# Layer 0 of a two-layer encoder trunk: the second half's squares, the logits' transposes and the first weight load are moved

## The chip, the cores and the metric

The kernel runs on one core of one Trainium2 chip. A core has five engines with a queue of instructions each: TensorE (PE in the profile; its weight loads are shown as PEld), VectorE (DVE), ScalarE (ACT), GpSimd (POOL) and SyncE (SP), which here issues the DMA loads. Each engine takes its queue strictly in order: an instruction that waits holds up all behind it. The metric is the device time of one execution in microseconds.

## The reference

The reference is a trunk of two layers over 1024 tokens of width 1024, all in float32. Layer 0 is the one that the change touches. Reduced to what matters here:

```
h     = rmsnorm(x, norm_mix_g[0])                 # needs the sum of squares of each token
proj  = h @ even_w_in                             # 28 blocks of 128 columns, and 8 logits per token
group A (RWKV-7): r, k, v, with token shift; decay, a and the gate g from low-rank products
                  g = sigmoid(xg @ g1) @ g2
group B (gated DeltaNet): q, k, v by a short convolution; gate
                  beta = sigmoid(logit 0..3);  g = -exp(a_log) * softplus(logit 4..7 + dt_bias)
mix   = concat(y_a, y_b) @ even_w_out
x     = x + mix; then a squared-ReLU MLP and a gated embedding
```

Layer 1 has windowed attention in place of the two groups. Nothing of what is computed changes.

## The kernel before

Activations lie transposed: 128 features on the partitions, tokens along the free axis. A product of full precision is made of three TensorE products of 128x128 by 128x512 each (high x high, high x low, low x high), so that a weight block of 128x1024 needs 8 x 3 = 24 matmuls for one half (HB = 512) of the tokens. `load_w` loads a weight (512 KB) into a buffer "wraw" (two of them), and `split_w` makes the two parts: a cast on ScalarE (L306) and a subtraction on VectorE (L307).

Layer 0 works in units. `layer0_in` lists 16 of them: for each half of the tokens, four pairs of an RWKV unit (two heads of group A) and a DeltaNet unit (one head of group B). Counted from 1, units 1, 3, 5, 7 of a half are RWKV and 2, 4, 6, 8 DeltaNet; the code counts u from 0. `l0_in` makes the input products of one unit after another. Its prologue, at u = 0 for the first half and u = 8 for the second, loads x, scales and splits it into `xg` (`split_scaled`, L355 and L356), sums its squares (`square`: ScalarE L666, and for all but the first tile an add on GpSimd L668), and then makes two low-rank products (`lora`) and the eight logits (`gdn_scalars`). In the first half the scaling by the token's norm is applied to the products when they are evacuated (`self.rs`), so that the first three products can begin before the norm is known; they lie in extra PSUM buffers until then.

`lora` mixes its weight on GpSimd twice (L700), splits both results, and makes two products. `gdn_scalars` loads the logits' weight, makes the product, evacuates it on VectorE (L717), transposes it on TensorE (L195) and computes beta and g with some two dozen small VectorE operations.

Behind the inputs, generators for `front`, `mid`, `back` and `post` of each unit (the lanes) are interleaved by `run`: it counts modelled time and asks next the lane that is due, with the estimates in `LAT`. `rwkv_front` and `gdn_front` make each unit's matrices; `inverse_start` sends the 16x16 diagonal blocks through memory to GpSimd, which inverts them in 28 small steps (L418, L420); `inverse_end` builds the full inverse on TensorE. A list scheduler then orders each engine's instructions: among those that its model holds ready it takes the one that stands first in the program, so that an instruction without early inputs can come much earlier in its queue than in the program.

The second half of x is needed twice: first for its sum of squares, in the program behind unit 7 (u == 6), then for the products of unit 9. The buffers for these loads, "ph" and "pl", hold two tiles each.

PSUM holds two buffers for these products (`bank`), taken in turn. The order in the program around the logits is: product of the logits, its transposes, first low-rank product of the gate (key "lg"), second.

## Time and profile before

| | us |
|---|---|
| median of 3 runs | 3081.69 |
| lowest and highest | 3079.91, 3084.43 |
| profiled execution | 3083.45 |
| its span on the core | 3081.7 |

| engine | busy us | share of the span |
|---|---|---|
| PE | 2969.4 | 96% |
| PEld | 2463.0 | 80% |
| DVE | 2233.0 | 72% |
| ACT | 1444.9 | 47% |
| POOL | 562.3 | 18% |

A row of a group or of the timeline names a line of the kernel, an engine and an operation, then the tile written and the tiles read (out<-in). In the timeline the first number is the start in us from the span's start, the second the duration, and the brackets at the end tell how long the engine had been idle and what ended that. In the view of waits each row gives who waited for whom, total us, how often, and the longest. A row of a line's own view gives shortest, median and longest duration in ns, and the first and last start. Layer 0's mixing takes about the first 900 us.

### The profile page before, as it was taken

To read this page: it belongs to the slowest core of one execution; us is meant where nothing else is said; L and a number is where in the kernel's file an instruction comes from. 1 tells how busy PE (TensorE), PEld (TensorE's weight loads), DVE (VectorE), ACT (ScalarE), POOL (GpSimd) and SP (SyncE) were. 2 spreads that over 40 slices of the span, in tenths; PEclk is the share of its full clock that TensorE was granted. 3 is DMA by queue.
4 is the path that set the end of the run, shared out by engine and by line. 5 is a ranking of instruction groups with operands and counts; after the bars stand their busy time and mean duration, and the time that the engine had idled before them with its cause. 6 is when DMAs were issued, how large, how long until landed. Compare 5 with 4: busy or idle time off the path is not lost.

```text
span 3081.7 us, 47201 instructions
## 1 busy us (share of the span) xinstructions
PE 2969.4 (96%) x17302; PEld 2463.0 (80%) x17302; DVE 2233.0 (72%) x4518; ACT 1444.9 (47%) x2824; POOL 562.3 (18%) x992
## 2 busy tenths in 40 slices
PE   7999999999999999999999989999999999999999
PEld 5777778777777888888888888989877888888887
DVE  6656766657848888878866677776868788878862
ACT  4333443334426544544433465666656544544431
POOL 6533542443500000000005111111200000000002
PEclk9999999999999999999999999999999999999999
DMA  4212112212346444754334111110256444754332
GB/s 139 71 54 62 55 55 74 62 53 64 120 158 215 160 154 149 252 174 149 126 101 131 55 44 41 49 55 27 78 190 227 144 154 150 258 168 152 124 109 99
DMA packets 190103, 362.18 MB, mean 118 GB/s; under 512 B 46272, under 2 KB 48560, under 8 KB 189872
## 3 DMA queue, kind: packets, MB, share of 16 engines
q1 hardware_dynamic: 161072, 306.73, 30.9%
q10 hardware_dynamic: 28800, 52.44, 4.4%
q8 instruction: 136, 2.23, 0.3%
q14 instruction: 95, 0.78, 0.1%
HBM read 265.71 MB, written 93.38 MB: 117 GB/s over the span
## 4 chain that ended last, share of the span: by engine, by line
PE 80%; DVE 9%; ACT 4%; DMA 3%; POOL 2%; issue 2%; SPq 0%; DVEq 0%; ACTq 0%; POOLq 0%
PE dps L180 66%; PE ch L180 2%; PE po L180 2%; PE pm L180 2%; PE pt L195 1%; PE iz L180 1%; PE sn L180 1%; PE tp L180 1%; DMA wraw<-in_w_qkv 1%; PE py L180 1%; POOL sub L420 1%; POOL subt L418 1%; PE pp L180 1%; DVE ptile L353 1%; DMA act<-in_w 1%
## 5 line engine op out<-in xcount | busy, mean ns | idle before, releaser
L180 PE MATMUL dps<-r,act 128*128 128x512 f32 x3528 | 829.1, 392 | 0.0
L180 PEld LDWEIGHTS dps<-r,act 128*128 128x128 f32 x3528 | 662.1, 188 | 145.7
L180 PE MATMUL dps<-xg,whi 128*128 128x512 f32 x1280 | 432.8, 418 | 14.2 <-ACT xg L355 7.3
L1617 POOL TENSOR_TENSOR pn<-pn,prs 128x512 f32<-128x512 f32 x32 | 46.9, 1468 | 1543.6 <-ACT prs L389 1449.0
L180 PE MATMUL dps<-wq,act 128*128 128x384 f32 x1536 | 305.4, 345 | 12.7 <-DVE vs L1879 7.1
L180 PEld LDWEIGHTS dps<-xg,whi 128*128 128x128 f32 x1280 | 233.5, 195 | 66.6 <-issue 8.0
L180 PEld LDWEIGHTS dps<-wq,act 128*128 128x128 f32 x1536 | 266.9, 191 | 16.0 <-DVE vs L1879 8.5
L180 PE MATMUL dps<-xg,wlo 128*128 128x512 f32 x640 | 258.0, 404 | 1.1 <-DVE wlo L307 1.1
L180 PE MATMUL dps<-late,act 128*128 128x512 f32 x960 | 229.2, 392 | 0.0
L180 PEld LDWEIGHTS dps<-late,act 128*128 128x128 f32 x960 | 180.3, 188 | 39.7
L1274 ACT CAST act<-act 128x512 fp32r<-128x512 f32 (+1 forms) x223 | 137.6, 648 | 130.9 <-PE dps L180 65.6
L1387 DVE TENSOR_TENSOR late<-late,dps 128x512 f32<-128x512 f32 x224 | 152.2, 684 | 56.1 <-PE dps L180 49.8
L1274 ACT CAST act<-late 128x512 fp32r<-128x512 f32 x210 | 124.3, 618 | 138.3 <-PE dps L180 94.7
L180 PE MATMUL dps<-act 128*128 128x512 f32 x672 | 165.0, 392 | 0.0
L1275 DVE TENSOR_TENSOR act<-act 128x512 fp32r<-128x512 f32 (+1 forms) x223 | 154.8, 722 | 5.2 <-ACT act L1274 5.1
L180 PEld LDWEIGHTS dps<-act 128*128 128x128 f32 x672 | 126.2, 188 | 28.6
L1275 DVE TENSOR_TENSOR act<-late,act 128x512 fp32r<-128x512 f32 x210 | 141.0, 688 | 8.9 <-ACT act L1274 7.0
L180 PEld LDWEIGHTS dps<-xg,wlo 128*128 128x128 f32 x640 | 124.1, 194 | 29.0 <-DVE wlo L307 1.6
L306 ACT CAST whi<-wraw 128x1024 fp32r<-128x1024 f32 x78 | 81.9, 1050 | 124.0 <-PE dps L180 79.8
L1525 DVE TENSOR_TENSOR xw<-xw,dps 128x512 f32<-128x512 f32 x174 | 118.0, 683 | 30.1 <-PE dps L180 27.8
L180 PE MATMUL dps<-xw,act 128*128 128x512 f32 x576 | 139.4, 392 | 0.0
L1392 ACT ACTIVATE late<-late 128x512 f32<-128x512 f32 x128 | 80.2, 629 | 112.5 <-DVE late L1387 107.7
(488 smaller groups left out, 5613.4 us busy)
## 6 DMA issues: line engine op xcount, KB each, us to landing
hb<-late ACTq DMA_DIRECT2D x168, 256.0 KB
act<-hb SPq DMA_DIRECT2D x138, 256.0 KB
late<-in_w SPq DMA_DIRECT2D x60, 512.0 KB
wraw<-in_w_in SPq DMA_DIRECT2D x56, 512.0 KB
act<-in_w SPq DMA_DIRECT2D x96, 256.0 KB
braw<-hb SPq DMA_DIRECT2D x72, 256.0 KB
wraw<-in_w_out SPq DMA_DIRECT2D x21, 512.0 KB
wraw<-in_w_qkv SPq DMA_DIRECT2D x21, 512.0 KB
```

The lines of the kernel that those rows point to most:

```text
L180: return self.begin(self.nc.tensor.matmul(out, lhsT, rhs, start=start, stop=stop, skip_group_check=again))
L195: return self.begin(self.nc.tensor.transpose(out, in_, ident))
L306: nc.scalar.copy(hi, raw)
L353: nc.vector.tensor_tensor(dst[:, 1, sl], src, dst[:, 0, sl].bitcast(F32), op=ALU.subtract)
L418: E.tensor_tensor(o, X[:, 0:i, i:i + 1].broadcast_to((NP, i, n)), Bq[:, i:i + 1, i + 1:16].broadcast_to((NP, i, n)), op=ALU.mult)
L420: E.tensor_tensor(X[:, 0:i, i + 1:16], X[:, 0:i, i + 1:16], o, op=ALU.add)
L1274: A.copy(hi, s)
L1275: V.tensor_tensor(lo, s, hi.bitcast(F32), op=ALU.subtract)
L1387: V.tensor_tensor(r, t, u, op=ALU.add)
L1392: A.activation(t, t, AF.Relu)
L1525: V.tensor_tensor(x[n][:, hs[hf]], x[n][:, hs[hf]], ps, op=ALU.add)
L1617: G.tensor_tensor(pn, pn, prs[:, sl], op=ALU.mult)
```

## The change

Four edits, all in the prologue of layer 0:

- The squares of the second half, which stood in the program behind unit 7, are spread: one load of two tiles and its two squares behind each of units 4 to 7 (u = 3 to 6). The load is pinned with `keep_in_program_order`, which draws an edge to the instruction traced last on its queue (SP), so that the scheduler can't issue it earlier. `load_x` gets an argument for that.
- `gdn_scalars` is cut in two. `gdn_logits` makes the product and its evacuation; the rest, from the transposes on, is called by `lora` between its first and its second product. The yield of "gdn_scalars0" goes.
- The first weight is loaded and split in two halves of its columns, 256 KB each: one before the first tile of x, one before the third.
- The loads of wa2, g2 and hv, and the exponential of a_log, come behind the three products of unit 1 in place of ahead of them.

```diff
                 if hf == 0:
                     acc = fr.tile([P, HB], F32, tag="rsbc", name="acc", bufs=2)
-                    self.w_first = self.load_w(a["w_in"][4])
+                    raw = self.wp.tile([P, 1024], F32, tag="wraw", name="wraw")
+                    self.w_first = [self.wp.tile([P, 1024], F32R, tag=f"w{q}", name=f"w{q}") for q in ("hi", "lo")]
+                    first = iter([slice(0, HB), slice(HB, T)])
...
                 for k in range(NK):
                     if hf == 0:
+                        if k % 2 == 0 and k < 4:
+                            c = next(first)
+                            nc.sync.dma_start(out=raw[:, c], in_=a["w_in"][4][:, c])
+                            self.split_w(raw[:, c], HB, [z[:, c] for z in self.w_first])
                         xr = self.t2()
                         nc.sync.dma_start(out=xr, in_=a["x"][k, :, 0:HB])
...
                 for f in squares:
                     f()
+                sc = {}
                 if hf == 0:
+                    rsc = self.sm.tile([P, 4], F32, tag="rsc", name="rsc")
+                    self.rs = fr.tile([P, HB], F32, tag="rsbc", name="rsbc", bufs=2)
+
+                    self.extra = [lambda t=t: self.psm.tile([P, HB], F32, tag=t, name="dps") for t in ("y", "ch", "pm")]
+                    self.late, self.plan = [], {2: lambda: self.row_stats([acc], rsc), 3: lambda: self.to_rows(rsc, self.rs)}
+                    raws = yield from getattr(self, nm + "_in")(p, hf, u)
                     self.wa2 = fr.tile([P, 512], F32, tag="wa2", name="wa2")
                     nc.sync.dma_start(out=self.wa2, in_=a["wa2"])
...
                     nc.scalar.activation(self.ea, self.hv[:, 0:1, :], AF.Exp)
-                sc = {}
-                if hf == 0:
-                    rsc = self.sm.tile([P, 4], F32, tag="rsc", name="rsc")
...
-                    raws = yield from getattr(self, nm + "_in")(p, hf, u)
...
             self.mark(("in", u), 1.0)
-            if u == 6:
-
-                acc = fr.tile([P, HB], F32, tag="rsbc", name="acc", bufs=2)
-                for q in range(4):
-                    x2 = self.load_x(q, self.pre, "pl" if q % 2 else "ph")
-                    for e in range(2):
-                        self.square(acc, x2[:, e], q + e == 0)
+            if 3 <= u < 7:
+
+                q = u - 3
+                if q == 0:
+                    acc = fr.tile([P, HB], F32, tag="rsbc", name="acc", bufs=2)
+                x2 = self.load_x(q, self.pre, "pl" if q % 2 else "ph", True)
+                for e in range(2):
+                    self.square(acc, x2[:, e], q + e == 0)
...
             if u % 8 == 0:
 
-                yield from self.gdn_scalars(hf, sc)
-                gg = yield from self.lora(1, [(0, 128, 2)], "lg")
+                ba = yield from self.gdn_logits()
+                gg = yield from self.lora(1, [(0, 128, 2)], "lg", lambda: self.gdn_scalars(hf, sc, ba))
...
-    def load_x(self, q, pool, tag):
+    def load_x(self, q, pool, tag, keep=False):
 
         x2 = pool.tile([P, 2, HB], F32, tag=tag, name="xr")
-        self.nc.sync.dma_start(out=x2, in_=self.a["x"][2 * q:2 * q + 2, :, HB:T].rearrange("k p t -> p k t"))
+        load = self.nc.sync.dma_start(out=x2, in_=self.a["x"][2 * q:2 * q + 2, :, HB:T].rearrange("k p t -> p k t"))
+        if keep:
+            self.tc.keep_in_program_order(load)
         return x2
...
-    def lora(self, i, mus, key):
+    def lora(self, i, mus, key, between=None):
...
         yield from self.dense_half(wa, lambda ps: nc.vector.tensor_tensor(out, ps, self.rs, op=ALU.mult))
+        if between is not None:
+            between()
         sb = yield from self.project(wb, key, 1)
...
-    def gdn_scalars(self, hf, sc):
-        nc, a, l0 = self.nc, self.a, self.l0
+    def gdn_logits(self):
+        nc, a = self.nc, self.a
...
         yield from self.dense_half(self.split_w(raw), lambda ps: nc.vector.tensor_tensor(ba[0:8, 0:HB], ps[0:8], self.rs[0:8],
                                                                                          op=ALU.mult))
-        yield "gdn_scalars0"
+        return ba
+
+    def gdn_scalars(self, hf, sc, ba):
+        nc = self.nc
         pt = self.bank()
```

4 lines of the change are left out of this document (removed).

## The prediction

> **What bounds the kernel now.** I read the page first, then a table of stretches around the one hole that the 40 slices show, then the waits of TensorE, then the rows around the hole.
>
> ```profile
> span 3081.7 us, 47201 instructions
> PE 2969.4 (96%) x17302; PEld 2463.0 (80%) x17302; DVE 2233.0 (72%) x4518; ACT 1444.9 (47%) x2824; POOL 562.3 (18%) x992
> ```
>
> TensorE works 96% of the span, so time is to be had only where it stands still or runs at half clock. The next table (columns: stretch, length, busy time of PE, PEld, DVE, ACT, POOL, granted clock, DMA share, GB/s) splits the 900 us of layer 0.
>
> ```profile
> 0.00:7.31 7.31, 0.00 (x0) 0.00 (x1) 1.24 (x4) 3.00 (x4) 6.33 (x58) 1.00 0.68 205
> 7.31:18.07 10.76, 9.33 (x27) 6.78 (x27) 8.87 (x11) 10.76 (x19) 10.14 (x23) 1.00 0.96 357
> 18.07:46.48 28.41, 28.41 (x130) 23.35 (x130) 15.10 (x22) 10.77 (x16) 22.09 (x20) 1.00 0.26 76
> 49.55:58.30 8.75, 0.00 (x2) 0.00 (x1) 7.50 (x19) 4.22 (x7) 5.38 (x5) 0.62 0.75 232
> 65.54:80.00 14.46, 13.03 (x68) 10.14 (x69) 7.25 (x29) 4.34 (x14) 0.50 (x1) 0.88 0.26 78
> 80.00:350.00 270.00, 261.39 (x2267) 200.92 (x2266) 171.27 (x377) 104.10 (x211) 121.66 (x270) 0.97 0.21 64
> 350.00:900.00 550.00, 526.14 (x4442) 407.47 (x4443) 365.00 (x831) 211.54 (x445) 217.14 (x471) 0.95 0.24 76
> ```
>
> Three idle places stand out: 7.31 us before the first matmul, 1.43 us inside the next 10.76, and 8.75 us in one piece from 49.55. The remaining 820 us of the layer hold 8.6 + 23.9 = 32.5 us, in crumbs. TensorE's waits of the first 90 us name what ended them:
>
> ```profile
> PE dps L195 <- DVE f L717: 8.7, 1, 8.7
> PE dps L180 <- ACT xg L355: 7.3, 1, 7.3
> PE dps L180 <- DVE wlo L307: 0.9, 1, 0.9
> ```
>
> The long wait is for the logits' evacuation (L717); the transposes of its result (L195) block TensorE's queue. The timeline around it, all engines mixed, shows why L717 is late:
>
> ```profile
> 39.10 1.83 POOL L668 TENSOR_TENSOR acc<-acc,xr 128x512 f32<-128x512 f32 x1
> 43.90 1.35 DVE L307 TENSOR_TENSOR wlo<-wraw,whi 128x1024 fp32r<-128x1024 f32 x1 [2.14 <-ACT whi L306]
> 46.51 1.26 POOL L668 TENSOR_TENSOR acc<-acc,xr 128x512 f32<-128x512 f32 x1
> 47.73 1.89 POOL L700 TENSOR_TENSOR wraw<-lraw,vecs 128x1024 f32<-128x1024 f32 x1
> 49.65 1.05 ACT L306 CAST whi<-wraw 128x1024 fp32r<-128x1024 f32 x1 [1.20 <-POOL wraw L700]
> 50.73 1.33 DVE L307 TENSOR_TENSOR wlo<-wraw,whi 128x1024 fp32r<-128x1024 f32 x1 [5.47 <-ACT whi L306]
> 57.57 0.67 DVE L717 TENSOR_TENSOR f<-dps,rsbc 8x512 f32<-8x512 f32 x1
> 58.30 0.59 PE L195 MATMUL dps<-ident,f 8*128 8x8 f32 x4 [8.75 <-DVE f L717]
> ```
>
> The logits' product was over by 46.48. VectorE stood idle for 5.47 us, not on L717 but on the weight split queued ahead of it (L307), which waits for ScalarE's cast, which waits for GpSimd's mixing of the second low-rank weight (L700), which stood behind a square sum of the second half (L668, acc<-acc,xr). After L307 VectorE works through unit 1's front until 57.57.
>
> **The change part by part.** Sums go against the profiled execution, 3083.45 us (its span 3081.7); the median of the three runs, 3081.69, is 1.76 lower.
>
> *First weight in halves.*
>
> ```profile
> 1.25 0.42 SPq L300 DMA_DIRECT2D wraw<-in_w_in  x1
> 3.58 0.20 POOL L241 TENSOR_SCALAR d_omu<-vecs 128x12 f32<-128x12 f32 x1
> 5.59 1.04 ACT L306 CAST whi<-wraw 128x1024 fp32r<-128x1024 f32 x1 [3.50 <-DMA wraw<-in_w_in]
> 6.54 0.72 ACT L355 ACTIVATE xg<-f,vecs 128x512 fp32r<-128x512 f32 x1
> 18.07 0.50 PE L180 MATMUL dps<-xg,wlo 128*128 128x512 f32 x1 [0.89 <-DVE wlo L307]
> 27.24 1.23 DVE L307 TENSOR_TENSOR wlo<-wraw,whi 128x1024 fp32r<-128x1024 f32 x1 [6.99 <-ACT whi L306]
> L666 ACT ACTIVATE xr<-xr x7: 613/617/633, 17.7 to 45.1; 128x512 f32<-128x512 f32 x7
> ```
>
> 512 KB took 4.3 us from issue (1.25) to cast (5.59). The 81.5 KB of the vectors, issued at 0.80, were used by 3.58, so 2.8 us. Between the two, 256 KB take about 3.4: the half lands near 4.7, 0.9 early. Its cast, half as wide, is near 0.62 (the row of ScalarE's 128x512 squares) for 1.04: 0.4 early. So the first matmul moves from 7.31 to about 6.0. Against it: two casts of 0.62 take 0.2 more of ScalarE, which has no idle time from 7.31 to 18.07 (10.76 busy of 10.76), and one more issue of 0.42 stands before the later x tiles. Bounds: a loss of 0.6, a gain of 2.5 (more than half of the 4.3 cannot go). The lead meets the fourth product's weight, whose split ends at 28.47; TensorE comes to it near 29.5 (24 matmuls a product at 0.227 us from 18.07, and 1 us of statistics), so about 1 us passes. I take **-1.0**.
>
> *wa2, g2, hv and the exponential behind unit 1's three products.* Three issues of 0.33 us on SP's queue leave the place ahead of the second weight and go ahead of the first low-rank load, which is in any case held to 18.04 by a buffer. The first reader of wa2 is at 46.60:
>
> ```profile
> 18.04 0.34 SPq L692 DMA_DIRECT2D lraw<-in_lora  x1
> 46.60 1.78 PE L180 MATMUL tp<-lao,wa 64*128 64x512 f32 x4
> ```
>
> Some 30 us cover a transfer; without that cover it would cost about its 3.4 us. Sum: **0**; the second weight comes some 2 us earlier, but its cast stands behind ScalarE's full queue.
>
> *Squares away from the start.* The eight squares of the second half leave ScalarE (8 x 0.62) and GpSimd (seven adds), and their loads SP's queue, where unit 2's weights stood behind them.
>
> ```profile
> L668 POOL TENSOR_TENSOR acc<-acc,xr x7: 1257/1305/2126, 35.2 to 51.0; 128x512 f32<-128x512 f32 x7
> L831 DVE TENSOR_SCALAR f<-f x8: 426/460/1404, 52.1 to 744.8; 128x512 f32<-128x512 f32 x8
> ```
>
> L700's second part can start 1.2 us earlier (the add at 46.51), and up to 3 if the add at 39.10 (1.83) goes from ahead of L700's first half, at 40.88, too. L831, the step between tanh and scan, lost 0.94 (1.404 against a median of 0.460) under the adds at 49.71. All of that lies ahead of L717.
>
> *Transposes behind the gate's low-rank product.* TensorE meets the 24 matmuls of that product first. Their weight is split by 45.25 (43.90 + 1.35), so they fill 24 x 0.227 = 5.45 us of the hole. Also, the product no longer needs the logits' PSUM buffer, which L717 holds. Left of the hole: 8.75 - 5.45 - (1.2 to 3) = 2.1 to 0.3; I take 1.2, so **-7.55**. What is late next is still L717, then the second low-rank product behind the transposes. The half-clock stretch after the hole goes as well:
>
> ```profile
> 58.82 1.22 PE L180 MATMUL dps<-xg,whi 128*128 128x512 f32 x2
> 61.55 0.79 PE L180 MATMUL dps<-xg,whi 128*128 128x512 f32 x2
> 62.18 0.39 PE L180 MATMUL dps<-xg,wlo 128*128 128x512 f32 x1
> 62.41 0.62 PE L180 MATMUL dps<-xg,whi 128*128 128x512 f32 x2
> ```
>
> From 58.82 to 61.95 seven matmuls start 0.43 apart, then 0.227 apart: 3.13 - 7 x 0.227 = **-1.5**. Does a 1.2 us rest of the hole keep a slow stretch alive? After the 1.43 us wait at 69.03 the row of 65.54:80.00 shows a clock of 0.88, which is (1 - 0.88) x 14.46 / 0.5 = 3.5 us at half speed, so here a short wait among small products was enough; kept, such a stretch would cost 1.7, and the time would be 1.7 higher. The Trainium skill, "TensorE: Matmul & The Clock Gate", Part 1, says that the gate halves the clock only after an idle window of some 3.4 us; by that rule the whole 1.5 is gained. The page and the 0.88 row differ, and the first hole, with its 0.62, suits both. I take the 1.5, since the matmuls now ahead are dense ones.
>
> The price: the second low-rank product now takes the PSUM buffer that the first one's evacuation has just to free, with only the 0.59 us transposes between.
>
> ```profile
> L706 DVE TENSOR_TENSOR lgo<-dps,rsbc x1: 683/683/683, 69.2 to 69.2; 128x512 f32<-128x512 f32 x1
> ```
>
> 0.68 + queueing - 0.59: from 0.1 to about 1.2 when L724 and a few of the gate's small VectorE steps are ahead; **+0.5**. In the second half (L717 at 460.6) other lanes' matmuls fill it: 0. The gate's scalars come 5.45 us later there and here; their reader, unit 2's front, comes after four more products (22 us), so 0.
>
> *Squares in units 4 to 7.* Each unit gets one load on SP's queue, two ScalarE squares and two GpSimd adds, beside the 16x16 inverses that GpSimd does. How much room has the inverse?
>
> ```profile
> 106.13 0.40 ACT L445 ACTIVATE T<-Xp,half 128x128 f32<-128x128 f32 x1 [6.42 <-DMA Xp<-z]
> 126.79 0.24 PE L180 MATMUL iz<-T,N 32*32 32x16 f32 x6
> 345.25 0.35 ACT L445 ACTIVATE T<-Xp,half 128x64 f32<-128x64 f32 x1 [0.45 <-DMA Xp<-z]
> 345.66 0.44 PE L180 MATMUL iz<-T,Ng 32*32 32x16 f32 x32
> ```
>
> Unit 1's result waits 20 us for TensorE, unit 6's none. Bounds: nothing (GpSimd is busy 121.66 of 270), and 4 x 2 x 1.305 = 10.4 if every add delays an inverse that TensorE awaits. Nearest is the row of the 270 us with 8.6 us of PE idle in all: I take a tenth, **+1.0**.
>
> Sum: -1.0 - 7.55 - 1.5 + 0.5 + 1.0 = -8.55; 3083.45 - 8.55 = 3074.9; on the footing of the median, **3073.1**.
>
> **The rivals.**
> *The hole moves on.* The products run ahead but the recurrent lanes do not, and TensorE waits later, where unit 6 has no room. For it: the pair of rows at 345. Against it: 20 us of room at unit 1, and GpSimd's chain moving up too. What stays is what the lanes gain (1.2 to 3 from L700, 0.94 from L831, say 3), the start's 1.0, less 1.5: 3081.69 - 2.5 = 3079.2.
> *Slower: GpSimd's adds hold up the inverses.* At units 4 to 7 each pair of adds takes up to 2 x 2.13 = 4.26 us, in the middle of the chain of 28 small steps; four of them, all awaited, are 17.0. Less the 9.55 of the other terms: 3081.69 + 7.5 = 3089.2. It decides from 15.7 us of delay on (3.9 a unit). Against it: the median add is 1.305, and unit 1's inverse has 20 us of room.
> *The pin doesn't hold*, and the squares still come early: the product fills 5.45, 3.3 us are left: -1.0 - 5.45 - 1.5 + 0.5 = -7.45, so 3074.2, inside the forecast.
>
> **How the numbers follow.** Forecast (with the pin's rival) 0.65, hole moves on 0.20, slower 0.13, still faster by more than 17 us 0.02. A change of 0.2% (6.2 us: 3075.5 and 3087.9) is about what a measurement of this kernel can tell from none. The forecast's own range is 3067 to 3077: all of the 8.75, 1.5 and 2.5 gained, or the start at its loss and a slow stretch kept. A new order of layer 0 can move its 32.5 us of crumbs by a few us either way, so it opens to 3065, and to 3084 to hold the second case; above that lies most of the slower one. Faster 0.66, same 0.21 (a hundredth of the forecast falls short of 3075.5), slower 0.13.
>
> **What would show it.** Right: first matmul near 6.0; no wait of TensorE above 2.5 us between 45 and 60, the low-rank product ahead of the L195 transposes; acc<-acc,xr on GpSimd only from about 150 us on; PE idle from 80 to 900 us within 4 us of 32.5. Wrong: waits for iz or T growing between 180 and 450, inverses stretched by adds, ScalarE waiting for an x tile in units 4 to 7.

## The result, and the profile after

The changed kernel is slower. Its median is 3095.16 us (3086.16 to 3105.72, nine runs) beside 3081.09 us for the kernel before (3075.65 to 3085.21, nine runs); the ratio is 1.0047, with a 95% interval of 1.0032 to 1.0061. The forecast was 3073.1, with a range of 3065 to 3084. All medians here and below are of fast executions; a slow one, of the kernel called before_squares below (10343 us at a mean granted clock of 0.497), is left out, and as it was the traced one, no trace of that kernel is read.

The page of the changed kernel, its span and its row of engines:

```profile
span 3093.3 us, 47222 instructions
PE 2980.7 (96%) x17302; PEld 2465.8 (80%) x17302; DVE 2233.5 (72%) x4519; ACT 1442.9 (47%) x2825; POOL 552.7 (18%) x992
```

Set this beside the rows of before. TensorE executes the same 17302 matmuls, and its idle time is the same: 3081.7 - 2969.4 = 112.3 us before, 3093.3 - 2980.7 = 112.6 after. Of the 11.6 us between the spans 11.3 are *busy* time. The same matmuls took longer, which is the mark of a lower granted clock, not of a wait.

The early part did most of what was forecast. The waits of TensorE in the first 80 us of the changed kernel (who waited for whom, total us, times, longest):

```profile
PE dps L179 <- ACT xg L354: 6.9, 1, 6.9
PE dps L194 <- DVE f L726: 2.3, 1, 2.3
...
PE dps L179 <- DVE wlo L306: 1.0, 1, 1.0
```

The hole of 8.75 us is down to 2.3. The timeline shows the low-rank product ahead of it and what comes after it:

```profile
54.38 0.39 PE L179 MATMUL dps<-xg,wlo 128*128 128x512 f32 x1
54.61 0.95 PE L179 MATMUL tp<-hsel,f 128*128 128x2 f32 x8
57.81 0.41 PE L194 MATMUL dps<-ident,f 8*128 8x8 f32 x4 [2.26 <-DVE f L726]
58.15 0.73 PE L179 MATMUL dps<-xg,whi 128*128 128x512 f32 x2
```

Where the time went is read from a table by stretches (length; busy time of PE, PEld, DVE, ACT, POOL; granted clock; DMA share; GB/s): the start, the rest of the first half's early units, the rest of layer 0, and layer 1 with the end. Before:

```profile
0.00:80.00 80.00, 60.85 (x262) 47.51 (x263) 46.86 (x94) 35.46 (x63) 52.55 (x110) 0.91 0.42 134
80.00:330.00 250.00, 241.90 (x2101) 187.08 (x2101) 156.35 (x347) 95.52 (x194) 106.33 (x235) 0.97 0.21 63
330.00:920.00 590.00, 565.20 (x4709) 437.68 (x4708) 391.44 (x882) 228.03 (x474) 232.47 (x505) 0.95 0.25 80
920.00:3065.00 2145.00, 2090.80 (x10190) 1782.28 (x10189) 1634.18 (x3190) 1084.36 (x2092) 169.63 (x141) 0.99 0.40 134
```

After:

```profile
0.00:80.00 80.00, 66.22 (x299) 50.90 (x300) 50.03 (x98) 34.27 (x60) 43.43 (x109) 0.98 0.32 101
80.00:330.00 250.00, 237.82 (x2008) 183.02 (x2008) 152.74 (x325) 92.39 (x187) 104.68 (x232) 0.91 0.22 66
330.00:920.00 590.00, 563.30 (x4722) 434.61 (x4718) 385.30 (x887) 225.65 (x476) 236.54 (x510) 0.95 0.25 79
920.00:3065.00 2145.00, 2090.41 (x10185) 1778.75 (x10184) 1638.50 (x3201) 1087.62 (x2098) 162.97 (x139) 0.99 0.40 135
```

Idle time is length less PE's busy time; time at half clock is (1 - clock) x length / 0.5. A us at half clock loses some 0.43 us among small matmuls (an estimate from clock_micro below, where 25.8 us of work took 44.6 to 46.8). So:

| stretch | idle, after less before | half clock, after less before | worth, us |
|---|---|---|---|
| 0 to 80 | 13.8 - 19.2 = -5.4 | 3 - 14 = -11 | -5.4 - 4.8 = -10.2 |
| 80 to 330 | 12.2 - 8.1 = +4.1 | 45 - 15 = +30 | +4.1 + 12.9 = +17.0 |
| 330 to 920 | 26.7 - 24.8 = +1.9 | 59 - 59 = 0 | +1.9 |
| 920 to 3065 | 54.6 - 54.2 = +0.4 | 43 - 43 = 0 | +0.4 |

The sum is +9.1 for a measured +11.6; the rest lies within what the clock's two decimals can hide. By this estimate the start gained 10 us, about what the prediction had for it, and the stretch from 80 to 330 us, where units 2 to 6 are at work, gave back 17, three quarters of it as half clock. The question is what put them there.

### The profile page after: what moved, and what is told of

Same layout as the page of the kernel before. It is cut to its first block, busy times and chain, and to the rows that moved or that the text cites. A ratio compares the mean times of both kernels' runs of the same rounds, so it can differ in the third digit from the quotient of the medians.

```text
span 3093.3 us, 47222 instructions
## 1 busy us (share of the span) xinstructions
PE 2980.7 (96%) x17302; PEld 2465.8 (80%) x17302; DVE 2233.5 (72%) x4519; ACT 1442.9 (47%) x2825; POOL 552.7 (18%) x992
## 4 chain that ended last, share of the span: by engine, by line
PE 81%; DVE 10%; ACT 3%; DMA 2%; issue 2%; POOL 2%; SPq 0%; ACTq 0%; DVEq 0%; POOLq 0%
PE dps L179 68%; PE ch L179 2%; PE po L179 2%; PE iz L179 1%; PE pt L194 1%; PE pm L179 1%; PE sn L179 1%; PE tp L179 1%; DVE wlo L306 1%; DVE ptile L352 1%; PE py L179 1%; DMA wraw<-in_w_qkv 1%; DVE f L1072 1%; POOL subt L417 1%; POOL sub L419 0%
## 5 line engine op out<-in xcount | busy, mean ns | idle before, releaser
L179 PEld LDWEIGHTS dps<-wq,act 128*128 128x128 f32 x1536 | 264.8, 189 | 17.0 <-DVE vs L1891 10.2
L305 ACT CAST whi<-wraw 128x1024 fp32r<-128x1024 f32 (+1 forms) x79 | 81.7, 1034 | 115.8 <-PE dps L179 79.6
```

Source lines behind the costliest of these rows:

```text
L179: return self.begin(self.nc.tensor.matmul(out, lhsT, rhs, start=start, stop=stop, skip_group_check=again))
L305: nc.scalar.copy(hi, raw)
```

## The experiments

The theories were these. **A**: the work of the squares in units 4 to 7 costs the time itself, either the GpSimd adds between the steps of the inverses (A1) or the loads and ScalarE's squares (A2). **B**: the new order of layer 0's instructions costs it, whichever edit brings the order about. **C**, formed later, is how B could cost so much: a short wait ahead of a stretch of small matmuls leaves that whole stretch at half clock. In what follows W is the first weight in halves, M the moved loads of wa2, g2 and hv, L the logits' transposes behind the low-rank product, S the squares in units 4 to 7. Ratios are to the kernel before, with their 95% intervals.

| kernel | contains | median, us | ratio |
|---|---|---|---|
| after | W M L S | 3095.16 | 1.0047 [1.0032, 1.0061] |
| after_no_squares | W M L | 3072.87 | 0.9978 [0.9965, 0.9991] |
| after_no_logits | W M S | 3102.85 | 1.0077 [1.0060, 1.0094] |
| before_logits | L | 3071.83 | 0.9979 [0.9961, 0.9998] |
| before_squares | S | 3104.54 | 1.0081 [1.0061, 1.0101] |
| before_halves | W | 3095.96 | 1.0050 [1.0028, 1.0072] |
| before_moves | M | 3087.73 | 1.0027 [1.0016, 1.0039] |
| after_no_adds | W M L S less the adds | 3084.42 | 1.0011 [0.9994, 1.0028] |
| after_adds_on_vector | adds on VectorE | 3082.76 | 1.0005 [0.9991, 1.0018] |
| after_loads_only | the loads and one square | 3077.23 | 0.9992 [0.9977, 1.0006] |
| after_unpinned | S without the pin | 3072.60 | 0.9975 [0.9959, 0.9991] |
| unpinned_again | the same | 3074.75 | 0.9979 [0.9964, 0.9995] |
| early_squares | S right behind unit 1 | 3087.87 | 1.0021 [1.0007, 1.0036] |
| dummy_adds | unpinned, and nine adds | 3084.28 | 1.0018 [1.0002, 1.0034] |

The kernel before had medians of 3078.3 to 3081.1 beside them.

### One part away, one part alone

**after_no_squares** puts the squares back behind unit 7, without the pin:

```diff
-            if 3 <= u < 7:
-                q = u - 3
...
-                x2 = self.load_x(q, self.pre, "pl" if q % 2 else "ph", True)
...
+            if u == 6:
+                acc = fr.tile([P, HB], F32, tag="rsbc", name="acc", bufs=2)
+                for q in range(4):
+                    x2 = self.load_x(q, self.pre, "pl" if q % 2 else "ph")
...
```

> The changed kernel with its squares put back: one block in the program behind unit 7, loads not pinned; the other three edits stay. Theory A (the pinned squares hold up GpSimd's inverses of units 2, 4 and 6, which took 6.5 to 10 us longer in the changed kernel): the loss goes with them, and the time falls to the kernel before or below it, 3070 to 3083. Theory B (any new order of layer 0 interleaves unit 3's front with unit 2's inverse and leaves TensorE runs of small matmuls, at half clock for 109 us of layer 0 against 85; the squares aren't the cause): it stays slow, 3088 to 3100, with more than 100 us at half clock.

**after_no_logits** takes the logits' part back:

```diff
-                ba = yield from self.gdn_logits()
-                gg = yield from self.lora(1, [(0, 128, 2)], "lg", lambda: self.gdn_scalars(hf, sc, ba))
+                yield from self.gdn_scalars(hf, sc)
+                gg = yield from self.lora(1, [(0, 128, 2)], "lg")
```

> The changed kernel with the logits' transposes back ahead of the gate's low-rank product; the other three edits stay. Theory A: as slow as the changed kernel or slower, since the squares stay, 3090 to 3102, and TensorE's hole near 50 us, 2.3 us in the changed kernel, is back at about 5 us (8.75 less the 1.2 to 3 of the absent squares). Theory B: the order changes again, so anything from 3078 to 3100; if the dense products' run ahead at 60 to 120 us is what starves later stretches, then 3078 to 3086.

**before_squares** and **before_logits** make these two edits alone in the kernel before (the same lines, the other way round).

> The kernel before with the pinned squares alone. Theory A: slower by 8 us or more, 3089 to 3098, with the inverses of units 2, 4 and 6 stretched. Theory B: within 6 us of before unless its order happens to change, and 3 us faster where the hole near 50 us shrinks with GpSimd's earlier low-rank weight.

> The kernel before with the logits' transposes behind the gate's low-rank product alone. Theory A: faster, 3072 to 3078: the hole of 8.75 us shrinks to about 3.3 and no square touches an inverse. Theory B: the products run ahead as in the changed kernel, later stretches lack them, and the gain is lost again: 3080 to 3095 with more time at half clock than the 85 us of before.

The squares are the loser and the logits the winner. With W, M and L the kernel takes 3072.87, within 0.3 us of the forecast for the whole change; that is in part luck, since the terms of W and L were not met one by one (see "Why the prediction was wrong"). The squares add 22.3 us to that (3095.16 - 3072.87), and alone about 25 (0.81% of 3080; 19 to 31). The logits' part gains 7.8 us alone (3079.62, the kernel before beside it, less 3071.83; by the interval of its ratio 0.6 to 12) and 7.7 in the company of the others (3102.85 - 3095.16).

The page of after_no_squares:

```profile
span 3065.3 us, 47212 instructions
PE 2961.1 (97%) x17302; PEld 2451.1 (80%) x17302; DVE 2227.9 (73%) x4519; ACT 1444.3 (47%) x2825; POOL 557.6 (18%) x992
```

This execution is 6 us below its kernel's median, so the sizes are rough. Idle 104.2 against 112.6 with the squares, busy 2961.1 against 2980.7: of 28.0 us between the two spans 8.4 are waiting and 19.6 are clock.

### What of the squares costs it

**after_adds_on_vector** and **after_no_adds** give `square` an engine for its sum, VectorE (`nc.vector`, shown here) or none (`None` in its place), for the second half alone (without the adds the sum of the squares is missing from the second half's norms):

```diff
-                    self.square(acc, x2[:, e], q + e == 0)
+                    self.square(acc, x2[:, e], q + e == 0, nc.vector)
```

> The changed kernel with the seven adds of the pinned squares on VectorE in place of GpSimd (0.68 us each there, 1.27 on GpSimd). Theory A1 (GpSimd is the contended engine: seven adds of 1.27 between the steps of the inverses, and VectorE slowed beside them): most of the 22 us that the squares cost goes, 3073 to 3082. Theory A2 (the loads' place on SP's queue or ScalarE's squares do it): 3090 to 3100. Theory B (a new order by itself costs or wins some 10 us): anything from 3075 to 3100.

> The changed kernel with those seven adds left out altogether (the second half's sum of squares then holds one tile of eight); loads and ScalarE's squares stay. Theory A1: as without the squares, 3070 to 3080, and the inverses of units 2, 4 and 6 take 28, 23 and 20 us again. Theory A2: 3090 to 3100.

**after_loads_only** keeps the four pinned loads and the first square (the second half's norms then hold one tile of eight):

```diff
                 for e in range(2):
-                    self.square(acc, x2[:, e], q + e == 0)
+                    if q + e == 0:
+                        self.square(acc, x2[:, e], q + e == 0)
```

> The changed kernel with the four pinned loads and one square alone; the other seven squares and the adds are left out (the second half's sum of squares then holds one tile of eight). Theory A1: 3070 to 3080. Theory A2 by the loads (each waits on SP's queue and holds up weights or the inverses' transfers behind it): 3090 to 3100; by ScalarE's squares: 3070 to 3080 here and 3090 to 3100 without the adds. Theory B: anything from 3070 to 3095, and not in step with what is left out.

**after_unpinned** lets the scheduler put the loads where it likes:

```diff
-                x2 = self.load_x(q, self.pre, "pl" if q % 2 else "ph", True)
+                x2 = self.load_x(q, self.pre, "pl" if q % 2 else "ph")
```

> The changed kernel with the same loads and squares in the same places of the program, but not pinned. The scheduler can then issue the first two loads early again, as in the kernel before. If the place in the queues costs: 3070 to 3080, with the first squares on GpSimd before 60 us. If the place in the program alone reorders layer 0: 3085 to 3100.

Taking the adds off GpSimd takes 12.4 us off the 22, leaving them out 10.7, and leaving out the other seven squares too another 7.2. The pinned loads with one square are still 4.4 above after_no_squares. A1 accounts for half, then, by this reading. The inverses do get stretched: the 28 steps on GpSimd that begin at 128 us take 26.8 us, for 20.6 in the unpinned kernel (from 126 us on), and those that begin at 233 us take 23.6, for 19.9 (from 221 us on). GpSimd in the changed kernel, with the adds (L675) among the steps of unit 4's inverse (L417, L419):

```profile
249.39 0.57 POOL L417 TENSOR_TENSOR subt<-sub,subb 32x36 f32<-32x36 f32 x1
249.93 1.27 POOL L675 TENSOR_TENSOR acc<-acc,xr 128x512 f32<-128x512 f32 x1
251.17 0.70 POOL L419 TENSOR_TENSOR sub<-sub,subt 32x36 f32<-32x36 f32 x1
...
251.97 1.27 POOL L675 TENSOR_TENSOR acc<-acc,xr 128x512 f32<-128x512 f32 x1
```

TensorE a little later:

```profile
258.42 0.62 PE L194 MATMUL pp<-ident,fr 128*128 128x128 f32 x4 [2.02 <-DVE fr L1197]
...
262.25 0.63 PE L179 MATMUL iz<-T,Ng 32*32 32x16 f32 x32 [2.21 <-ACT T L444]
262.81 2.07 PE L179 MATMUL tp<-AR,b 64*128 64x128 f32 x14
```

The same operations in the unpinned kernel, where TensorE doesn't wait:

```profile
250.41 0.38 PE L179 MATMUL iz<-T,Ng 32*32 32x16 f32 x24
250.72 1.16 PE L179 MATMUL tp<-AR,b 64*128 64x128 f32 x14
```

The wait for that inverse is 2.21 us, and the 14 transposes behind it take 2.07 us in place of 1.16. Stretched inverses were one of the signs that the prediction had named as wrong. Their waits are small beside 22 us, though, and the second effect, the slow matmuls, is not in the prediction's price for it. Nor do the adds alone make this wait: in early_squares (below), without an add near, TensorE waits 1.33 us at the same place.

The unpinned kernel also shows the rival in which the pin doesn't hold. Its squares run at 37 to 53 us, as before; those of the changed kernel run at 132 to 350. First the unpinned kernel's line of the adds, then the changed one's:

```profile
L675 POOL TENSOR_TENSOR acc<-acc,xr x7: 1274/1289/2155, 37.0 to 52.9; 128x512 f32<-128x512 f32 x7
```

```profile
L675 POOL TENSOR_TENSOR acc<-acc,xr x7: 1254/1272/1289, 132.1 to 350.4; 128x512 f32<-128x512 f32 x7
```

With its 3072.6 the unpinned kernel beats both.

### The squares elsewhere, other work in their place, and the weight alone

**early_squares** keeps pin and squares, but puts all four loads behind unit 1's gate product:

```diff
                 self.mark(("lg", hf))
+                if hf == 0:
+                    acc = fr.tile([P, HB], F32, tag="rsbc", name="acc", bufs=2)
+                    for q in range(4):
+                        x2 = self.load_x(q, self.pre, "pl" if q % 2 else "ph", True)
+                        for e in range(2):
+                            self.square(acc, x2[:, e], q + e == 0)
```

> The changed kernel with all four pinned loads and their squares right behind the gate's second low-rank product of unit 1, not in units 4 to 7. GpSimd has 10 us of idle time there (69.8 to 78.4 us in the changed kernel, before the first inverse) and no inverse is under way. Theory A1 (the squares cost because of where they meet the inverses and unit 3's and later fronts; out of the way of the low-rank weight they shorten the hole of 5.6 us near 56 us to 2.3): 3066 to 3072, below every kernel so far. If the squares cost wherever they are pinned: 3078 to 3095.

**dummy_adds** takes the unpinned kernel and gives GpSimd nine adds that nothing needs, behind units 4 to 7:

```diff
+            if 3 <= u < 7:
+                if u == 3:
+                    dum = fr.tile([P, 384], F32, tag="dum", name="dum")
+                    nc.gpsimd.memset(dum, 0.0)
+                for j in range(3 if u == 6 else 2):
+                    nc.gpsimd.tensor_tensor(dum, dum, raws[j][:, 0:384], op=ALU.add)
```

> The changed kernel without the pins (3072.6, squares early), plus nine adds of 128x384 on GpSimd that nothing reads, two or three behind each of units 4 to 7, each waiting for that unit's own products: about 9 us of GpSimd work in the places of the pinned adds, with no load and no ScalarE square. Theory A1 (GpSimd's time among the inverses is the main price, some 11 of 22 us): 3080 to 3088. If the pinned adds cost only together with the loads and squares that they wait for: 3070 to 3076.

**before_halves** is the first weight in two halves, alone in the kernel before:

```diff
-                    self.w_first = self.load_w(a["w_in"][4])
+                    raw = self.wp.tile([P, 1024], F32, tag="wraw", name="wraw")
...
+                        if k % 2 == 0 and k < 4:
+                            c = next(first)
+                            nc.sync.dma_start(out=raw[:, c], in_=a["w_in"][4][:, c])
+                            self.split_w(raw[:, c], HB, [z[:, c] for z in self.w_first])
```

> The kernel before with the first weight loaded and split in two halves, alone. The prediction's term is 1.0 us gained. The traces of the changed kernels show the first matmul at 6.8 to 7.3 us for 7.31, but the second product's wait for its weight ending at 18.2 to 18.9 for 18.07, so the expectation now is no gain: within 4 us of before, 3077 to 3085.

The dummy adds cost 11.7 us (3084.28 - 3072.60), as A1 asks. The other two do not fit it. The early squares have their adds at 103 to 115 us, none in units 4 to 7, and are still 15 us above the unpinned kernel. And the halved weight, which puts nothing at all among the lanes, costs 15 us alone (0.50%; 0.28 to 0.72%). Its row of engines:

```profile
PE 2988.2 (96%) x17302; PEld 2472.4 (80%) x17302; DVE 2231.3 (72%) x4519; ACT 1445.0 (47%) x2825; POOL 555.1 (18%) x992
```

Its span is 3099.8, so it idles 111.6 us, 0.7 less than before, and is busy 18.8 longer. TensorE's instruction order differs from that of before from 25.5 us on, though only the first load was touched, since the list scheduler works out every queue anew. So there the order alone did it, by way of the clock.

Taken over ten of the profiles, busy time goes with the mean granted clock, for the same 17302 matmuls: 2961.1 at 0.982 (after_no_squares), 2965.5 at 0.980 (after_unpinned), 2969.4 at 0.978 (before), 2974.0 at 0.976 (after_adds_on_vector), 2978.4 at 0.975 (after_no_adds), 2980.7 at 0.974 (after), 2987.2 at 0.973 (after_no_logits), 2988.2 at 0.972 (before_halves). Two of the others stand off this line, 2968.0 (before_logits) and 2978.1 (early_squares), both at 0.977.

### Is it the clock, and what sets it?

One place gave the hint. The same run of 232 small and dense matmuls of the lanes took 18.2 us at full clock in the unpinned kernel (from 249.66 us on) and 31.3 us, nearly all of it at half clock, in early_squares (from 255.18 us on), where a 1.33 us wait stood shortly ahead of it. The next runs asked whether that is the cause, whether slow places belong to the order, and whether an edit without any work shifts the time.

**clock_micro** is a kernel of its own: dense matmuls, a wait for a chain of VectorE operations, then a stretch of small ones:

```diff
+        for turn in range(3):
+            for waits in (0, 1, 2, 4):
+                d = dense(60)
+                first = raw
+                if waits:
+                    first = sb.tile([P, HB], F32, tag="chain", name="chain", bufs=2)
+                    nc.vector.tensor_scalar(first, d, 0.5, None, op0=mybir.AluOpType.mult)
+                    for _ in range(waits - 1):
+                        nc.vector.tensor_scalar(first, first, 0.5, None, op0=mybir.AluOpType.mult)
+                lanes(8, first)
```

> This kernel computes nothing of the trunk; it only measures the clock. Twelve turns (0, 1, 2 and 4 chained 128x512 VectorE operations, three times over): 60 dense 128x512 matmuls, then TensorE waits for the chain, then some 216 small matmuls like those of the lanes, with no further wait. Theory C (a stretch of small matmuls keeps the clock that it enters with, and a wait of 1 to 3 us ahead of it is enough to enter slow): turns without a wait run their small matmuls at a clock of 1.0; turns with the longer waits run them at 0.5 for most or all of the stretch, so that the same stretch takes up to 1.7 times as long; dense matmuls bring the clock back. Rival D (the clock follows the kind of matmul, not the wait): all twelve stretches show the same clock. Rival E (only idle time above some 3 us counts): stretches behind waits of up to 2.6 us show 1.0, all of them.

Four of its waits in the timeline, of three sizes:

```profile
60.49 0.37 PE L17 MATMUL pm<-raw,chain 64*128 64x128 f32 x1 [0.78 <-DVE chain L61]
...
101.36 0.37 PE L17 MATMUL pm<-raw,chain 64*128 64x128 f32 x1 [1.25 <-DVE chain L63]
...
143.13 0.37 PE L17 MATMUL pm<-raw,chain 64*128 64x128 f32 x1 [2.17 <-DVE chain L63]
...
283.86 0.37 PE L17 MATMUL pm<-raw,chain 64*128 64x128 f32 x1 [1.24 <-DVE chain L63]
```

The stretches behind them, and the first one, without a wait:

```profile
20.15:45.86 25.71, 25.71 (x434) 23.55 (x433) 0.00 (x0) 0.00 (x0) 1.00 0.01 3
60.49:86.27 25.78, 25.78 (x433) 23.62 (x433) 0.00 (x0) 0.00 (x0) 1.00 0.01 2
101.36:127.13 25.77, 25.77 (x433) 23.62 (x433) 0.00 (x0) 0.00 (x0) 1.00 0.01 2
143.13:187.77 44.64, 44.64 (x433) 40.85 (x433) 0.00 (x0) 0.00 (x0) 0.53 0.01 1
...
283.86:329.23 45.37, 45.37 (x433) 41.58 (x433) 0.00 (x0) 0.00 (x0) 0.52 0.01 1
```

The same 432 small matmuls take 25.8 us or 45 us. There is nothing between: the clock is 1.00, or 0.50 to 0.53 for the stretch. Of three stretches each, none was slow behind no wait, none behind 0.78 us, one behind 1.24 us, and all three behind 2.17 us. Each slow stretch had TensorE busy for all of its 45 us, and the clock came back only 1.3 to 4.2 us into the dense matmuls that followed. So rivals D (the kind of matmul alone) and E (only idle time above 3 us) both fall: these small matmuls keep the clock that they are left with behind the wait, and a wait of 1.2 to 2.2 us can decide it.

The wait's length isn't all, though. In the clock's records every change lies on a raster, a fixed grid in time, of 3.41 us (the stretches at half clock inside the kernels last 3.4, 6.8, 10.2 us and so on). Of the three waits of 1.24 or 1.25 us the slow one lies wholly between two points of it, and the other two are cut by one, at 101.22 and 490.34 us. Where a wait falls on the raster is thus a rival to its length for the single cases; no run varied the two apart.

**early_again** and **after_again** are the same programs once more, for their traces (no edit).

> The kernel with all four loads and squares early, once more. Theory C: the stretch of lanes that took 30.9 us from 255 us on at half clock, and 18.2 us at full clock in the unpinned kernel, follows a wait of TensorE of 1.3 us there, and is slow again if that wait is there again. Rival: it runs at full clock this time, with the same wait, so that the wait is not what sets it.

> The changed kernel once more, for its trace. Theory C: where the places at half clock come back (144, 175, 189, 250, 261, 353 us), they belong to the order of the instructions and to its waits; stretches that differ between the two traces of the same program say how much of the 0.6% spread of its times is clock. Rival (the earlier trace was an accident): half clock between 80 and 330 us near the 17 to 21 us of the faster kernels, in place of 44.

early_squares and early_again have the same matmuls in the same order at this place. The wait was 1.33 us the first time and 0.88 the second. First early_squares, its timeline and the stretch to 290 us:

```profile
254.01 0.24 PE L179 MATMUL iz<-T,Ng 32*32 32x16 f32 x4 [1.33 <-ACT T L444]
...
255.34 1.11 PE L179 MATMUL ch<-W,F 128*128 128x64 f32 x4
256.39 0.52 PE L179 MATMUL iz<-T,Ng 32*32 32x16 f32 x24
```

```profile
254.01:290.00 35.99, 35.99 (x264) 26.82 (x265) 10.50 (x24) 6.95 (x22) 8.81 (x32) 0.57 0.13 40
```

Then early_again:

```profile
254.18 0.24 PE L179 MATMUL iz<-T,Ng 32*32 32x16 f32 x4 [0.88 <-ACT T L444]
...
255.51 0.66 PE L179 MATMUL ch<-W,F 128*128 128x64 f32 x4
256.10 0.38 PE L179 MATMUL iz<-T,Ng 32*32 32x16 f32 x24
```

```profile
254.18:290.00 35.82, 35.58 (x403) 27.61 (x403) 16.23 (x44) 11.15 (x30) 11.55 (x39) 1.00 0.22 64
```

By 290 us the one has executed 264 matmuls and the other 403, with no idle time in the first and 0.24 us in the second. The first execution took 3090.74 us, the second 3081.24. The slow stretch, 30.7 us at half clock by the clock's records, is worth some 13 us at 0.43 each, so it alone is enough for the difference. That the 0.45 us more of waiting made it is likely from clock_micro, but one pair of executions doesn't show it.

In after_again the slow places came back where they were: the clock's records give half clock at 142, 179, 193, 261 and 357 us, against 144, 175, 189, 250 and 261, and 353 the first time, besides others of 3.4 us; between 80 and 330 us 48 us in all, against 44 (the unpinned kernel 20, before 17). So in the changed kernel they belong to its order and not to one execution.

Do they stand behind waits? In the changed kernel those at 138, 144, 175 and 261 us begin in one or right behind it, 27 of the 44 us: waits of 1.62 and 2.58 us end at 137.09 and 143.24, one of 1.99 at 175.97, and one of 2.21 at 262.25 (shown above). Two of the rows:

```profile
143.24 0.69 PE L179 MATMUL iz<-X,T 32*32 32x32 f32 x32 [2.58 <-DVE T L468]
...
175.97 0.48 PE L179 MATMUL ch<-b,tm 128*64 128x64 f32 x4 [1.99 <-DVE U L986]
```

The one at 189 us does not. TensorE has no idle time in the 4.8 us ahead of it, nor in the slow 10.2 us (columns as in the tables by stretches above):

```profile
184.00:188.80 4.80, 4.80 (x44) 3.40 (x43) 1.89 (x4) 1.67 (x4) 1.21 (x4) 1.00 0.13 27
188.80:199.00 10.20, 10.20 (x48) 7.93 (x49) 6.13 (x26) 1.80 (x5) 0.77 (x2) 0.50 0.09 14
```

The kernel before has the same place, 10.2 us from 184.8 us on. The matmuls ahead of it are small ones, among them eight of a single column (128x1), a kind that clock_micro doesn't have. So most of the half clock that the change added stands at waits, as theory C asks, but not every slow place does: some stretches of small matmuls lose the clock without any wait.

**before_moves** moves the loads of wa2, g2, hv and the exponential behind unit 1's products, alone in the kernel before:

```diff
+                    raws = yield from getattr(self, nm + "_in")(p, hf, u)
                     self.wa2 = fr.tile([P, 512], F32, tag="wa2", name="wa2")
                     nc.sync.dma_start(out=self.wa2, in_=a["wa2"])
...
-                    raws = yield from getattr(self, nm + "_in")(p, hf, u)
```

> The kernel before with the fourth edit alone: the loads of wa2, g2 and hv, and the exponential, behind unit 1's three products. No square, no logit and no first load is moved, and no work is added. My prediction: 0, so 3077 to 3083 against a kernel before near 3080. Theory B (any new order of layer 0 falls into other waits and other stretches at half clock): 3 to 15 us off in either direction, with a sum of half clock in layer 0 that goes with it, about 0.5 us of time for each us. Theory A (only GpSimd's adds and squares cost): within 2 us of the kernel before.

It is slower by 0.27% (0.16 to 0.39%), some 8 us, though it adds no work and moves no square. Its profiled execution took 3082.86, the fastest of its ten runs, so the trace shows little of that loss: 111.0 us idle and 2970.0 busy, as before. That the 8 us are clock is argued from the others, not shown.

### How many dense matmuls bring the clock back?

**clock_dense_first** waits 2.17 us each time and then puts dense matmuls ahead of the small ones:

```diff
+            for ahead in (0, 4, 12, 30):
+                d = dense(60)
...
+                mm(pm[:, 0:P], first[0:64, 0:P], raw[0:64, P:2 * P], start=True, stop=True)
+                if ahead:
+                    dense(ahead)
+                lanes(8, raw)
```

> Computes nothing of the trunk. Twelve turns, each: 60 dense matmuls, a wait of some 2.2 us (four chained VectorE operations), one small matmul that ends the wait, then 0, 4, 12 or 30 dense 128x512 matmuls, then the stretch of 432 small ones, which takes 25.8 us at full and 45 us at half clock. My prediction counted on this: dense matmuls behind a wait restore the clock. If it holds: the turns with 0 run slow (45 us), as behind the 2.2 us waits before; those with 30 (6.8 us at full, up to 13.6 at half clock) run at 25.8; the turns with 4 and 12 tell how many are needed (the dense stretches that followed slow ones got the clock back after 1.7 to 4.6 us, so 12, at 2.7 to 5.4 us, should be near the border). If dense matmuls restore nothing while small ones follow, all twelve are slow.

The stretches of small matmuls behind 0, 4 and 12 dense ones, first turn, and behind 4 in the second:

```profile
23.21:69.20 45.99, 45.99 (x434) 42.09 (x432) 0.00 (x0) 0.00 (x0) 0.50 0.01 1
87.84:133.97 46.13, 46.13 (x433) 42.25 (x433) 0.00 (x0) 0.00 (x0) 0.51 0.00 1
154.49:180.19 25.70, 25.70 (x433) 23.55 (x433) 0.00 (x0) 0.00 (x0) 1.00 0.01 2
...
312.20:337.91 25.71, 25.71 (x434) 23.56 (x433) 0.00 (x0) 0.00 (x0) 1.00 0.01 2
```

Slow were three of three without dense matmuls, two of three behind 4, none behind 12 and none behind 30. What the dense matmuls did is seen between the wait and the small ones. The first row is the four of the first turn, the second the twelve of the second:

```profile
86.23:87.84 1.61, 1.61 (x7) 1.04 (x7) 0.00 (x0) 0.00 (x0) 1.00 0.00 0
...
353.90:358.85 4.95, 4.95 (x14) 3.60 (x14) 0.00 (x0) 0.00 (x0) 0.66 0.00 0
```

The four ran at full clock, and it fell only behind them, at 88.4 us. So they are no test of bringing it back: in two turns it fell behind the four, in the third it didn't fall. Of the six turns with 12 or 30 dense matmuls it fell in four, for one record of 3.4 us each, and was back before the small ones began; in the other two it didn't fall. Twelve dense matmuls, 3.0 us at full clock and 4.5 to 4.6 where it fell, were enough each time.

**unpinned_again** repeats after_unpinned with more rounds.

> The changed kernel without the pin, again, with more rounds: 0.9975 [0.9959, 0.9991] before. If the gain is real, below 1 again, with 0.998 the middle of what is expected; theory C takes the time of this order from its 84 to 90 us at half clock in layer 0 and the shorter hole, so 3070 to 3077 beside a kernel before near 3080.

It is below 1 again, 0.9979 with 0.9964 to 0.9995. The change without its pin is the version that is faster than both kernels.

## Why the prediction was wrong

By its own steps:

- **Squares in units 4 to 7, +1.0 (0 to 10.4): this step failed.** They cost 22.3 us in the company of the others, about 25 alone. The bound was every add delaying an awaited inverse, eight times 1.3 us, and a tenth of it was taken; it priced waiting alone. Between the profiles with and without the squares, 28.0 us apart (the latter ran 6 us under its median), there are 8.4 us of idle time, under the bound of 10.4, and on top of it 19.6 us of lower clock, which the bound did not hold. In the changed kernel 27 of the 44 us at half clock between 80 and 330 us stand at waits of 1.6 to 2.6 us, as told above.
- **The slower rival, 3089.2, had the right sign and mechanism in part.** It priced the adds at 17.0 us in the inverses. Removing the adds, or putting them on VectorE, gives back 10.7 and 12.4; the remaining 10 to 12 us are the other squares, the loads and the order. It had a chance of 0.13, and it too counted waiting alone.
- **Transposes behind the gate's low-rank product, -7.55, slow stretch -1.5, buffer +0.5: near in sum, -8.55 against a measured -7.7 to -7.8, and in part by luck.** Inside it three sizes were off. Alone, the product fills 2.8 us of the hole and not 5.45 (8.75 to 5.96 in the kernel with this part alone), because L717's counterpart comes 3.0 us later there (its transposes start at 61.29, against 58.30). Taking the squares away from the start then shortens it by 3.4 to 3.7 (5.7 with W, M and L, 2.3 with the squares moved as well), not 1.2 to 3. The rest left in the hole was 2.26, for 1.2 forecast. And the 1.5 us of the slow stretch were not gained in the profiled execution: from 59.10 to 62.50 us, behind the 2.26 us wait and among the dense matmuls of the second low-rank product, the clock is at 0.51, which is the case that the prediction priced at 1.7 (in after_again it falls only at 70.3 us). With L alone it is at 0.51 for 6.3 us behind the hole, from 61.81 on. Of the 9.8 us between the profiles of before and before_logits the first 80 us hold 4.2 of idle time and 3.4 us less at half clock; the rest comes later, with an order that no term priced. No wait for the buffer shows: the next product starts at 58.15, right behind the transposes.
- **The rivals of the other kind.** That the pin doesn't hold was put at 3074.2; without it the kernel took 3072.6 and 3074.75, so that sum was right, for a kernel in which it is so, though the hole kept 5.6 us there and not 3.3, so that the number is in part luck. That the hole moves on (3079.2) didn't happen: without the squares the logits' gain stays.
- **First weight in halves, -1.0: not confirmed.** The first matmul moved from 7.31 to 6.95, not to 6.0, and TensorE then waited 1.0 us for the second weight as before. In the whole with M and L it changed nothing that could be measured (0.9978 with W and M, 0.9979 without). Alone it cost 15 us, far outside its bounds of -2.5 to +0.6, and through the clock.
- **Moved loads, 0: right beside L, wrong alone (+8).** The transfers were hidden, as argued; what was not counted is that the edit re-orders layer 0.
- **"A new order of layer 0 can move its 32.5 us of crumbs by a few us either way": this was too small by a factor of several.** The idle crumbs did move by a few us (from 32.5 to 38.2 between 80 and 900 us, where within 4 was forecast). The clock moved by twice as much (12.9 us in the table above). W, M, S and L alone give +15, +8, +25 and -7 us, +41 in sum; together they gave +14, and W, M and L without S gave -7, as L alone. The parts don't add up, because each order falls into other short waits, as far as the traces show.
- **The clock.** The prediction met the effect at one place, the row of 65.54:80.00 with its clock of 0.88 after a 1.43 us wait, worked out 3.5 us at half speed from it, and set it against the Trainium skill, "TensorE: Matmul & The Clock Gate", Part 1, by which the clock falls after an idle window of some 3.4 us. It took the gain that the rule gives for the one stretch behind the hole, and no such price anywhere else. The row was the better guide: 1.24 us was enough once in three, 2.17 us six times in six with small matmuls right behind. The first hole doesn't suit that rule either, as the prediction had it: a clock of 0.62 over 8.75 us is 6.65 us at half, so that it fell 2.1 us into the hole. The reason given for the gain, that the matmuls behind are dense ones, holds by half: 12 dense ones restore the clock, but they don't keep it from falling for 3.4 us, as at 59.10 us. The same section of the Trainium skill says that some 3.4 us of sustained work bring the full clock back; here that holds for dense matmuls, and not for the small ones of clock_micro, which stayed slow through 46.8 us of work without a gap.

Of the signs named ahead, the adds came where forecast (from 132 us on, 150 was named), the hole's wait was 2.26 (below 2.5), and the inverses were stretched, which was a sign of being wrong. TensorE's waits for T, another such sign, did not grow where it was named: between 180 and 450 us they are 2.8 us in sum, for 3.1 before. They grew ahead of that, so that from 80 to 450 us they are 7.0 for 5.0.

One question stays open. The adds cost 10 to 12 us in three comparisons (each uncertain by some 6 to 7 by the intervals), but re-orderings without any added work cost 8 and 15, and every variant was scheduled anew. So how much of the 22 us is the squares' own and how much is the luck of this order isn't settled; an order held fixed with only the squares inserted wasn't tried.

## What to carry to other kernels

When a kernel keeps TensorE 96% busy, compare its busy time for the same matmuls before its waits: here the idle time was equal to 0.3 us, and the loss was clock. In clock_micro and clock_dense_first a wait of 1.2 to 2.2 us cost at most 3.4 us at half clock ahead of a dozen dense matmuls, and up to 20 us of time ahead of a long stretch of small ones. So where a wait can't be avoided, a dozen dense matmuls behind it are worth a try; in this kernel it wasn't tried. And where a scheduler works out every queue anew, try each edit alone and in company: single edits of no weight moved this kernel by 8 to 15 us, and their sum said little about the whole.

## What was not expected of the hardware

- The same 432 small matmuls took 25.8 us or 44.6 to 46.8 us, with TensorE busy throughout, depending on a wait of 1.24 to 2.17 us ahead of them; 0.78 us did nothing in three tries. The clock changes on a raster of 3.41 us only.
- The half clock didn't end by itself under the small matmuls of clock_micro. It lasted up to 51 us there, and ended 1.3 to 4.2 us into the dense matmuls; in early_squares it lasted 30.7 us.
- Nor does it always need a wait to begin: at 188.8 us it began in the changed kernel with TensorE busy throughout the 4.8 us ahead.
- One program's own spread is this effect too. Of the changed kernel's nine runs the fastest, 3086.16 us, had a mean clock of 0.979, and the slowest, 3105.72, 0.971: 8 thousandths of 3095 us are 50 us more at half clock, which at 0.43 is 21 us, for a measured 19.6.
